# Two transformer blocks on one core: paired heads and earlier transposes in the sliding attention, another order of the dense products, no weight splits on GpSimd, and a paired operand for gate and up

## The chip, the cores and the metric

One NeuronCore of a Trainium2 chip runs the whole program in one launch. The metric is the device time of one execution in microseconds, the median of a few runs. The engines are named as in the profile: PE (TensorE, matrix products) with its weight loads as PEld, DVE (VectorE), ACT (ScalarE), POOL (GpSimd) and SP (SyncE, which issues the transfers).

## The reference, cut to what matters

The first block (a gated mixer with a delta rule, then a mixture of 32 experts) is not touched. The change lies in the second block: two layers, each an attention mixer with a residual and a SwiGLU with a residual, on 256 positions of width 1024.

```
for layer in range(2):
    hn = rmsnorm(h, attn_norm[layer])
    if layer % 2 == 0:   # 8 low-rank heads (96 wide, rotary) and 8 dilated heads (64 wide)
        mix = even_mixer(hn, e_w_in, e_q_norm, e_kv_norm, e_w_uq, e_w_ukv, e_w_out, ...)
    else:                # 16 query heads on 2 key heads (64 wide), window 128, one sink a head
        mix = odd_mixer(hn, o_w_qkv, o_sinks, o_w_out, ...)
    h = h + mix
    gu = rmsnorm(h, ffn_norm[layer]) @ w_gate_up          # 1024 -> 2 * 2816
    h = h + (silu(gu[..., :2816]) * gu[..., 2816:]) @ w_down
return rmsnorm(h, final_norm)
```

In the odd mixer, query heads 0 to 7 use key head 0 and query heads 8 to 15 use key head 1.

## The kernel before, in words

Everything is float32 in memory. For the dense products each operand is split into a high part, rounded to fp32r, and a low part, the remainder: `split` (L247) lets ACT write the high part and DVE (or another engine that it is given) subtract for the low part. A product is then three matmuls: high by high, high by low, low by high.

`dense` (L277) makes one such product. It fetches weights through SP in pieces of 2048 columns into `raw` (a ring of five), splits them 512 columns at a time into `wh` and `wl` (five buffers each, pool `sp`), and accumulates in one of two PSUM tiles `pd`. In mode "fm" the weights are the stationary operand and the 256 positions stream by: three matmuls of 256 columns (L309, L311, L312) for each 128 x 128 piece of weights. In mode "tm" the positions are stationary and 512 columns of weights stream by (L319 to L321). The argument `lo_eng` names another engine for some of the low parts; `block2` gives every fourth to POOL (`lo_p`).

`Norm` (L1162) turns a residual into transposed operands `xh` and `xl` (eight chunks of 128 features) and computes the reciprocal root mean square `rs` separately; `finish` also spreads it along a row (`rb`, matmuls L1196, copy L1199). The factor is applied only when a product leaves PSUM (`evac_row`, `evac_col`).

`attention` (L1201) works on four heads at a time. Two heads share a step: scores into PSUM (L1217), then on DVE, for each head and each half of the queries, scale and add the table of the mask (L1221, L1222) and take the maximum (L1223, L1224); ACT makes the exponentials with their sums (L1234); POOL normalizes the first 128 columns (L1241) and DVE the other 256 (L1242). The returned `out` does the rest for each pair of heads: three transposes a head (L1251), a copy out of PSUM on ACT (L1253), the products with the values (L1257), and a split. A plain f32 matmul shows in the trace as two matmuls.

`block2` puts it together. Even layer: the low-rank inputs `e_a` (416 columns), a chain of small steps on them (squares, a root, rotary, scaling, transposes L1379, splits), then dilated keys `e_b[0]`, low-rank keys, queries, scores of low-rank heads 0 to 3, their values, scores of heads 4 to 7, dilated queries `e_b[2]`, and the rest; dilated values `e_b[1]` and the first half of the output product `e_out` come behind the last scores. Odd layer: keys `o_kv` (256 columns, each key head twice, so that a query head in either half of the partitions finds its key beside it), values `o_v`, queries `o_q[0]`, scores, queries `o_q[1]`, and so on.

`ffn` (L1263) makes gate and up in eleven steps of 512 columns (256 of gate, 256 of up; mode "fm"), with the factor, the silu, the product and a split behind each, and then the down product in mode "tm".

The order of instructions on each engine is not written out: a scheduler fixes it when the program is built, from the order of the code, declared priorities and its own estimate of when operands are ready. Each engine then executes its own list in that order.

## Time and profile before

| what | us |
|---|---|
| three runs | 1402.52, 1404.14, 1411.59 (median 1404.14) |
| the profiled execution | 1411.76, of which the span is 1410.0 |
| PE busy in it | 1237.7 (88% of the span) |
| DVE, ACT, POOL busy in it | 722.3, 576.6, 122.1 |

The profile is of one execution. A busy time is the union of the instructions of an engine; the ends of matmuls are modelled, so the distance from one matmul's start to the next says more of the rate than its duration does. An idle time of an engine is put down to what released it last. Times of rows are counted from the start of the span.

### The profile page before, as it was taken

What the parts mean: (1) busy time and instruction counts of PE and PEld (TensorE: products, weight loads), DVE (VectorE), ACT (ScalarE), POOL (GpSimd) and SP (SyncE); (2) the same over time, 40 slices, a digit from 0 to 9 for tenths busy, and PEclk for the clock granted to TensorE, in tenths of its full rate; (3) what the DMA queues carried; (4) which work ended last, traced back from release to release, by engine and by line L of the source; (5) the groups of instructions that cost most, each with busy time, mean ns of one, the idle gap of its engine ahead of it and who ended that gap; (6) DMA issues with size and microseconds to landing.
All of it is one profiled execution on the core that took longest, in us unless ns stands there. A gap on an engine that the chain in (4) does not pass through costs nothing.

```text
span 1410.0 us, 26508 instructions
## 1 busy us (share of the span) xinstructions
PE 1237.7 (88%) x10876; PEld 1003.3 (71%) x10877; DVE 722.3 (51%) x1485; ACT 576.6 (41%) x1138; POOL 122.1 (9%) x108
## 2 busy tenths in 40 slices
PE   5999999999788666877777579999999999999997
PEld 4997988998555242443434268689998896999985
DVE  6997945886331010110100198666665668666664
ACT  3776534643211010110101156665555547655553
POOL 2431100030000000000000023300000014000000
PEclk9999988999899888888878789999999999999999
DMA  7453652687899999999999934335555542555550
GB/s 277 150 180 105 191 169 76 223 342 296 336 426 424 426 419 426 426 426 426 425 426 426 403 139 162 137 130 179 180 183 192 184 175 91 172 187 181 179 180 30
DMA packets 58973, 356.15 MB, mean 253 GB/s; under 512 B 13312, under 2 KB 13824, under 8 KB 17632
## 3 DMA queue, kind: packets, MB, share of 16 engines
q1 hardware_dynamic: 57072, 346.96, 64.5%
q0 software_dynamic: 1488, 6.92, 1.3%
q8 instruction: 87, 1.43, 0.4%
q10 hardware_dynamic: 288, 0.52, 0.1%
q14 instruction: 38, 0.31, 0.1%
HBM read 352.55 MB, written 1.84 MB: 251 GB/s over the span
## 4 chain that ended last, share of the span: by engine, by line
PE 36%; DMA 19%; DVE 5%; ACT 3%; issue 1%; POOL 1%; SPq 0%; DVEq 0%; ACTq 0%
DMA xw<-in_w_dram 15%; PE pd L311 7%; PE pd L312 7%; PE pd L309 7%; DMA raw<-in_w_dram 4%; PE pd L320 4%; PE pd L319 4%; PE pd L321 4%; ACT s L1234 1%; PE ps L1257 1%; DVE wl L249 1%; PE ps L1217 1%; PE ps L1251 1%; PE ps L1040 0%; PE ps L1025 0%
## 5 line engine op out<-in xcount | busy, mean ns | idle before, releaser
L248 ACT ACTIVATE wh<-raw 128x512 fp32r<-128x512 f32 (+1 forms) x532 | 330.8, 630 | 317.0 <-PE pd L311 166.6
L249 DVE TENSOR_TENSOR wl<-raw,wh 128x512 fp32r<-128x512 f32 x497 | 362.9, 738 | 182.8 <-ACT wh L248 181.8
L312 PE MATMUL pd<-xh,wl 128*128 128x256 f32 x1232 | 351.1, 285 | 3.9 <-DVE wl L249 2.3
L309 PE MATMUL pd<-xh,wh 128*128 128x256 f32 x1232 | 351.2, 285 | 0.4 <-ACT vn L737 0.4
L311 PE MATMUL pd<-xl,wh 128*128 128x256 f32 x1232 | 350.2, 284 | 0.0
L312 PEld LDWEIGHTS pd<-xh,wl 128*128 128x128 f32 x1232 | 236.8, 192 | 7.1 <-DVE wl L249 3.3
L309 PEld LDWEIGHTS pd<-xh,wh 128*128 128x128 f32 x1232 | 237.0, 192 | 3.0 <-issue 1.6
L311 PEld LDWEIGHTS pd<-xl,wh 128*128 128x128 f32 x1232 | 237.0, 192 | 1.6 <-issue 1.2
L1029 DVE COPY hs<-ps 128x256 f32<-128x256 f32 x32 | 13.6, 425 | 294.8 <-PE ps L1025 294.8
L1025 PE MATMUL ps<-xw,xe 128*32 128x256 f32 x1568 | 106.8, 405 | 36.6 <-DMA xw<-in_w_dram 32.7
L249 POOL TENSOR_TENSOR wl<-raw,wh 128x512 fp32r<-128x512 f32 (+1 forms) x35 | 57.6, 1646 | 636.9 <-ACT wh L248 616.1
L1025 PEld LDWEIGHTS ps<-xw,xe 128*32 128x32 f32 x1568 | 48.8, 115 | 88.1 <-DMA xw<-in_w_dram 47.1
L1035 ACT ACTIVATE hx<-ps 128x128 f32<-128x128 f32 x32 | 8.9, 277 | 244.3 <-PE ps L1032 244.3
L1040 PE MATMUL ps<-xw,hx 128*32 128x256 f32 x784 | 62.6, 457 | 21.6 <-DVE hx L1036 16.7
L320 PE MATMUL pd<-wl,hh 128*128 128x512 f32 x176 | 68.6, 390 | 0.0
L321 PE MATMUL pd<-wh,hl 128*128 128x512 f32 x176 | 68.6, 390 | 0.0
L319 PE MATMUL pd<-wh,hh 128*128 128x512 f32 x176 | 68.5, 389 | 0.0
L1040 PEld LDWEIGHTS ps<-xw,hx 128*32 128x32 f32 x784 | 24.4, 125 | 50.5 <-DVE hx L1036 23.1
L320 PE MATMUL pd<-wl,xh 128*128 128x512 f32 (+2 forms) x144 | 55.7, 387 | 2.5 <-DVE wl L249 2.5
L1047 PE MATMUL pd<-ys,owt 32*128 32x256 f32 x512 | 43.3, 459 | 16.2 <-ACT ys L1044 10.2
L321 PE MATMUL pd<-wh,xl 128*128 128x512 f32 (+2 forms) x144 | 54.3, 377 | 1.2 <-DVE xl L275 1.2
L319 PE MATMUL pd<-wh,xh 128*128 128x512 f32 (+2 forms) x144 | 54.7, 380 | 0.0
(451 smaller groups left out, 1750.4 us busy)
## 6 DMA issues: line engine op xcount, KB each, us to landing
xw<-in_w_dram SPq DMA_DIRECT2D x147, 1024.0 KB, 19.6
raw<-in_w_dram SPq DMA_DIRECT2D x45, 1024.0 KB, 19.6
raw<-in_gu_dram SPq DMA_DIRECT2D x44, 1024.0 KB, 5.1
raw<-in_w_in_dram SPq DMA_DIRECT2D x32, 1024.0 KB, 5.1
raw<-in_dn_dram SPq DMA_DIRECT2D x20, 1024.0 KB, 4.9
raw<-in_e_b_dram SPq DMA_DIRECT2D x6, 1024.0 KB, 5.1
bc<-in_big_dram POOLq DMA_DIRECT2D x8, 512.0 KB, 6.6
raw<-in_w_pb_dram SPq DMA_DIRECT2D x4, 1024.0 KB, 5.3
```

Source lines behind the costliest of these rows:

```text
L248: self.nc.scalar.activation(hi, src, AF.Copy)
L249: (eng or self.nc.vector).tensor_tensor(lo, src, hi.bitcast(F32), op=OP.subtract)
L309: nc.tensor.matmul(o, a, xh[:, kc, :], start=(kc == 0 and oc % 2 == 0), stop=False, skip_group_check=True)
L311: nc.tensor.matmul(o, a, xl[:, kc, :], start=False, stop=False, skip_group_check=True)
L312: nc.tensor.matmul(o, b, xh[:, kc, :], start=False, stop=(kc == nk - 1), skip_group_check=True)
L319: nc.tensor.matmul(o, xh[:, kc, ts], a, start=(kc == 0), stop=False, skip_group_check=True)
L320: nc.tensor.matmul(o, xh[:, kc, ts], b, start=False, stop=False, skip_group_check=True)
L321: nc.tensor.matmul(o, xl[:, kc, ts], a, start=False, stop=(kc == nk - 1), skip_group_check=True)
L1025: T.matmul(ph[32 * c:32 * c + 32, :256], xe[:, kc, ei * 32:ei * 32 + 32], wt[kc // 2][:, kc % 2, c * 256:(c + 1) * 256], start=(kc == 0), ...
L1040: T.matmul(py[32 * c:32 * c + 32, :256], hx[:, fc % 2, (fc // 2) * 32:(fc // 2) * 32 + 32], wt[4 + fc // 2][:, fc % 2, c * 256:(c + 1) * 2 ...
L1047: T.matmul(total(c, t), owt[32 * c:32 * c + 32, ei, t * 128:(t + 1) * 128], ys[32 * c:32 * c + 32], start=(e == 0 and t == 0), stop=(e == ...
L1217: T.matmul(ps[:, t * 128:t * 128 + 128 * (t + 1)], q[:, t * 128:t * 128 + 128], k[:, :128 * (t + 1)], start=(t == 0 and j == 0), stop=(j = ...
```

## The change

In the feed-forward step, the normalized operand is stored with its high and low parts side by side for each chunk (`x2`, a new pool), and a new mode "fm2" streams both, 512 columns, past the high weights in one matmul, and the high part alone, 256 columns, past the low weights. Gate and up are made in 22 steps of 256 columns. The two halves of the wide sum are joined when they leave PSUM: ACT copies one, DVE adds the other. Weights are split 1024 columns at a time, with three buffers of each kind instead of five, through the down product too.

In the even layer the order becomes: dilated keys (left in PSUM), low-rank inputs, the row of the factor, dilated queries, then the low-rank chain; dilated values stand where dilated queries stood. In the odd layer the first queries come ahead of keys and values, and the sixteen heads are reordered as 0, 8, 1, 9, ..., so that both heads of a pair use different key heads and the keys need only 128 columns. No weight split goes to POOL in this block. In `attention` the maxima of two heads are one instruction each, the second normalization goes from DVE to ACT, the transposes of the next pair stand ahead of the products of this one, one of two copies out of PSUM goes to DVE, and the products of a pair alternate between the halves of the array in another order. The end of the expert stage no longer makes the row of the factor.

```diff
@@ layout
+PAIRED = np.arange(16).reshape(2, 8).T.ravel()
...
-    o["o_kv"] = _tiles(w, [np.concatenate([r(1024, 1088), r(1024, 1088), r(1088, 1152), r(1088, 1152)])], 8)[0]
+    o["o_k"] = _tiles(w, [r(1024, 1152)], 8)[0]
@@ dense
-        step = max(1, 512 // ncol)
+        step = max(1, self.wide // ncol)
...
-                wh = self.sp.tile([128, 512], F32R, name="wh", tag="wh")
-                wl = self.sp.tile([128, 512], F32R, name="wl", tag="wl")
+                wh = self.sp.tile([128, self.wide], F32R, name="wh", tag="wh")
+                wl = self.sp.tile([128, self.wide], F32R, name="wl", tag="wl")
...
+                    if mode == "fm2":
+                        for oc in range(ncol // 128):
+                            c = c0 + oc * 128
+                            nc.tensor.matmul(ps[:, oc * 512:(oc + 1) * 512], wh[:, c:c + 128],
+                                             xh[:, kc].rearrange("p a b -> p (a b)"), start=(kc == 0), stop=False,
+                                             skip_group_check=True)
+                            nc.tensor.matmul(ps[:, oc * 512:oc * 512 + 256], wl[:, c:c + 128], xh[:, kc, 0], start=False,
+                                             stop=(kc == nk - 1), skip_group_check=True)
@@ end of moe
-                x.finish()
+                x.finish(False)
@@ attention
-                V.tensor_reduce(mx[:, 0, i:i + 1], s[:, i, :128], AX.X, OP.max)
-                V.tensor_reduce(mx[:, 1, i:i + 1], s[:, i, 128:], AX.X, OP.max)
+            V.tensor_reduce(mx[:, 0, i0:i0 + wide], s[:, i0:i0 + wide, :128], AX.X, OP.max)
+            V.tensor_reduce(mx[:, 1, i0:i0 + wide], s[:, i0:i0 + wide, 128:], AX.X, OP.max)
...
-            V.tensor_scalar(s[:, i, 128:], s[:, i, 128:], den[:, 1, i:i + 1], None, op0=OP.mult)
+            S.activation(s[:, i, 128:], s[:, i, 128:], AF.Copy, scale=den[:, 1, i:i + 1])
...
+        def turned(i2):
...
+                if i == i2:
+                    S.activation(d, pp[:, :384], AF.Copy)
+                else:
+                    V.tensor_copy(d, pp[:, :384])
...
+            nxt = turned(0)
             for i2 in range(0, n, 2):
+                pT, nxt = nxt, turned(i2 + 2) if i2 + 2 < n else None
...
-                for kb in range(2):
-                    for i in (i2, i2 + 1):
-                        r = slice(64 * (i - i2), 64 * (i - i2) + 64)
-                        T.matmul(po[r, kb * 128:256], vv(heads[i], kb), pT[i][:, kb * 256:256 + kb * 128], start=(kb == 0),
-                                 stop=(kb == 1), skip_group_check=True)
+                for i, kb in ((0, 1), (1, 0), (0, 0), (1, 1)):
+                    T.matmul(po[64 * i:64 * i + 64, kb * 128:256], vv(heads[i2 + i], kb), pT[i][:, kb * 256:256 + kb * 128],
+                             start=(kb != i), stop=(kb == i), skip_group_check=True)
@@ ffn
+        sp, self.wide = self.sp, 1024
+        with tc.tile_pool(name="ffn", bufs=1) as fp, tc.tile_pool(name="ffw", bufs=2) as fw, \
+                tc.tile_pool(name="ffs", bufs=3) as self.sp:
...
-            for s in range(11):
+            for s in range(22):
...
+                    lo = self.work.tile([128, 2, 256], F32, name="tf", tag="tf")
+                    nc.scalar.activation(lo, p2[:, :, 1], AF.Copy)
+                    nc.vector.tensor_tensor(gu[0][:, :, s % 2], p2[:, :, 0], lo, op=OP.add)
...
-                self.dense(A[f"gu{i}"][s], 512, 8, x.xh, x.xl, "fm", act)
+                self.dense(A[f"gu{i}"][s], 256, 8, x.x2, None, "fm2", act)
@@ block2, even
+                pk = self.dense(A["e_b"][0], 512, 8, x.xh, x.xl, "fm", None)
...
-                self.dense(A["e_a"], 416, 8, x.xh, x.xl, "tm", self.evac_col(ca[:, :, :416], x.rs), lo_p)
+                self.dense(A["e_a"], 416, 8, x.xh, x.xl, "tm", self.evac_col(ca[:, :, :416], x.rs))
+                x.row()
+                self.evac_row(kb, x.rb)(pk)
+                qb = self.x2.tile([128, 8, 256], F32, name="qb", tag="x2")[:, :4]
+                self.dense(A["e_b"][2], 512, 8, x.xh, x.xl, "fm", self.evac(qb))
...
-                self.dense(A["e_b"][0], 512, 8, x.xh, x.xl, "fm", self.evac_row(kb, x.rb), lo_p)
...
-                self.dense(A["e_b"][2], 512, 8, x.xh, x.xl, "fm", self.evac(qb), lo_p)
+                self.dense(A["e_b"][1], 512, 8, x.xh, x.xl, "tm", self.evac_col(vb, x.rs))
...
-                self.dense(A["e_b"][1], 512, 8, x.xh, x.xl, "tm", self.evac_col(vb, x.rs), lo_p)
@@ block2, odd
-                self.dense(A["o_kv"], 256, 8, x.xh, x.xl, "fm", self.evac_row(kk, x.rb), lo_p)
-                self.dense(A["o_v"], 128, 8, x.xh, x.xl, "tm", self.evac_col(vs, x.rs), lo_p)
-                self.dense(A["o_q"][0], 512, 8, x.xh, x.xl, "fm", self.evac(q[:, :4]), lo_p)
+                self.dense(A["o_q"][0], 512, 8, x.xh, x.xl, "fm", self.evac(q[:, :4]))
+                self.dense(A["o_k"], 128, 8, x.xh, x.xl, "fm",
+                           lambda ps: V.tensor_tensor(kk, ps[:, :256], x.rb, op=OP.mult))
+                self.dense(A["o_v"], 128, 8, x.xh, x.xl, "tm", self.evac_col(vs, x.rs))
```

## Rows read from the trace of the kernel before

**Rows 1.** Windows: length, then busy us of PE, PEld, DVE, ACT, POOL; clock; DMA

```profile
814.60:933.40 118.80, 107.36 (x663) 90.34 (x664) 91.63 (x218) 72.46 (x183) 33.70 (x29) 0.98 0.39 135
815.00:860.00 45.00, 38.06 (x254) 35.65 (x253) 43.06 (x98) 23.53 (x51) 11.69 (x6) 0.95 0.48 171
933.40:1061.70 128.30, 128.09 (x1068) 127.87 (x1067) 84.58 (x138) 71.94 (x117) 0.00 (x0) 1.00 0.54 181
1061.70:1122.30 60.60, 60.60 (x275) 50.21 (x274) 34.78 (x53) 31.87 (x54) 0.00 (x0) 1.00 0.53 182
1122.30:1210.90 88.60, 85.76 (x583) 71.09 (x582) 61.92 (x168) 54.95 (x150) 24.25 (x26) 1.00 0.41 144
```

**Rows 2.** Waits of PE in 812 to 935: total us, times, longest

```profile
PE ps L1196 <- DVE rs L1192: 2.1, 1, 2.1
PE ps L1379 <- DVE ca L1367: 1.6, 1, 1.6
PE pd L312 <- POOL wl L249: 1.6, 1, 1.6
PE pd L309 <- DVE kb L1317: 1.2, 1, 1.2
PE pd L320 <- POOL wl L249: 0.8, 1, 0.8
PE ps L1257 <- ACT pT L1253: 0.8, 1, 0.8
```

**Rows 3.** Waits of PE in 1121 to 1215, the same columns

```profile
PE ps L1257 <- ACT pT L1253: 1.5, 2, 0.8
```

**Rows 4.** Windows of PE alone, inside gate and up, and inside down

```profile
960.00:1050.00 90.00, 90.00 (x752) 1.00 0.56 186
1100.00:1120.00 20.00, 20.00 (x90) 1.00 0.57 197
```

**Rows 5.** Chain of work that ended last, even layer: start us, us, what

```profile
817.73 0.57 ACT xh L271
...
833.85 0.62 ACT ca L1325
...
841.54 0.30 PE ps L1379
...
856.32 2.62 PE ps L1217 x16
```

**Rows 6.** Timeline of PE around one pair of heads: start us, us, instruction, idle before

```profile
1167.50 1.24 PE L1257 MATMUL ps<-pT,vs 128*64 128x256 f32 x8 [0.81 <-ACT pT L1253]
1168.67 0.87 PE L1251 MATMUL ps<-cst,s 128*128 128x128 f32 x6
```

**Rows 7.** Timeline, a split on POOL and the VectorE instruction beside it

```profile
830.60 1.36 POOL L249 TENSOR_TENSOR wl<-raw,wh 128x512 fp32r<-128x512 f32 x1 [1.09 <-ACT wh L248]
...
830.72 1.26 DVE L218 TENSOR_SCALAR nr_y<-nr_t 128x2 int32<-128x2 int32 x1
```

**Rows 8.** Groups by line, whole span: busy us, mean ns of one, idle before

```profile
L249 DVE TENSOR_TENSOR wl<-raw,wh 128x512 fp32r<-128x512 f32 x497 | 362.9, 738 | 182.8 <-ACT wh L248 181.8
L248 ACT ACTIVATE wh<-raw 128x512 fp32r<-128x512 f32 (+1 forms) x532 | 330.8, 630 | 317.0 <-PE pd L311 166.6 <-DVE wl L249 72.2 <-PE pd L321 54.8
L1242 DVE TENSOR_SCALAR s<-s,den 128x256 f32<-128x256 f32 x32 | 11.0, 405 | 0.2
L1253 ACT ACTIVATE pT<-ps 128x384 f32<-128x384 f32 x32 | 14.3, 486 | 7.2 <-PE ps L1251 6.9
L1014 ACT ACTIVATE owt<-ps 128x512 f32<-128x512 f32 x16 | 9.6, 597 | 1.1
L807 DVE TENSOR_TENSOR tf<-pd,ga 128x512 f32<-128x512 f32 x4 | 2.6, 687 | 0.4 <-PE pd L312 0.4
L1071 DVE TENSOR_TENSOR acc<-acc,bc 128x1024 f32<-128x1024 f32 x2 | 2.4, 1214 | 0.0
L885 ACT ACTIVATE h<-h,nmean,nr_y 128x1024 f32<-128x1024 f32 x2 | 2.4, 1232 | 1.9 <-DVE nmean L878 1.9
```

More of the change, by code (lines that the diff above doesn't have):

```diff
@@ L125, in layout @@
             ("norm", g["dn_norm_w"][0]), ("b_r", np.concatenate([g["b_rg"][0], g["b_re"][0]])),
-            ("sink", g["o_sinks_2"][0])]
+            ("sink", g["o_sinks_2"][0][PAIRED])]
     n = 0
@@ L322, in dense @@
                                              skip_group_check=True)
-        if k_to == nk:
+        if k_to == nk and consume is not None:
             consume(ps)
@@ L376, in run @@
             self.work = pool("work", 2)
-            self.sp = pool("sp", 5)
+            self.sp, self.wide = pool("sp", 5), 512
+            self.x2 = pool("x2")
             self.block2(x, n)
@@ L385, in mixer @@
         sp_es = ExitStack()
-        self.sp = sp_es.enter_context(tc.tile_pool(name="sp", bufs=5))
+        self.sp, self.wide = sp_es.enter_context(tc.tile_pool(name="sp", bufs=5)), 512
         self.ln_norm(h, h, 1e-5)
@@ L1165, with __init__ @@
     class Norm:
-        def __init__(self, p, h, gain):
+        def __init__(self, p, h, gain, paired=False):
             self.p, self.h, self.gain = p, h, gain
-            self.xh = p.act.tile([128, 8, 256], F32R, name="xh", tag="xh")
-            self.xl = p.act.tile([128, 8, 256], F32R, name="xl", tag="xl")
+            if paired:
+                self.x2 = p.x2.tile([128, 8, 2, 256], F32R, name="x2", tag="x2")
+                self.xh, self.xl = self.x2[:, :, 0], self.x2[:, :, 1]
+            else:
+                self.xh = p.act.tile([128, 8, 256], F32R, name="xh", tag="xh")
+                self.xl = p.act.tile([128, 8, 256], F32R, name="xl", tag="xl")
             self.ss = p.small.tile([128, 2, 2], F32, name="nss", tag="nss")
@@ L1193, in finish, with row @@
             if row:
-                ps = p.pt.tile([128, 512], F32, name="ps", tag="ps")
-                for t in range(2):
-                    nc.tensor.matmul(ps[:, t * 128:(t + 1) * 128], self.rs[:, t:t + 1].to_broadcast([128, 128]),
-                                     p.cs("ident"), start=True, stop=True, skip_group_check=True)
-                self.rb = p.small.tile([128, 256], F32, name="rb", tag="rb")
-                nc.vector.tensor_copy(self.rb, ps[:, :256])
+                self.row()
+        def row(self):
+            p, nc = self.p, self.p.nc
+            ps = p.pt.tile([128, 512], F32, name="ps", tag="ps")
+            for t in range(2):
+                nc.tensor.matmul(ps[:, t * 128:(t + 1) * 128], self.rs[:, t:t + 1].to_broadcast([128, 128]),
+                                 p.cs("ident"), start=True, stop=True, skip_group_check=True)
+            self.rb = p.small.tile([128, 256], F32, name="rb", tag="rb")
+            nc.vector.tensor_copy(self.rb, ps[:, :256])
     def attention(self, heads, qk, vv, tab, scale, oh, ol, sink=None, wide=2):
@@ L1285, in ffn @@
                     done(s)
+        self.sp, self.wide = sp, 512
         if nx is not None:
@@ L1332, in block2 @@
         ident, small = self.cs("ident"), self.small
-        lo_p = lambda i: P if i % 4 == 3 else None
         if True:
@@ L1367, in block2 @@
                     V.tensor_scalar(ca[:, t, 256:384], ca[:, t, 256:384], rs[:, 2 * t + 1:2 * t + 2], None, op0=OP.mult)
-                cxh = ev.tile([128, 3, 256], F32R, name="cxh")
-                cxl = ev.tile([128, 3, 256], F32R, name="cxl")
+                cx = ev.tile([128, 2, 3, 256], F32R, name="cx")
+                cxh, cxl = cx[:, 0], cx[:, 1]
                 krT = ev.tile([128, 256], F32, name="krT", tag="kr")
@@ L1389, in block2 @@
                 va = ev.tile([128, 2, 512], F32, name="va")
-                kb = ev.tile([128, 4, 256], F32, name="kb")
                 vb = ev.tile([128, 2, 512], F32, name="vb", tag="ca")
-                qb = ev.tile([128, 4, 256], F32, name="qb")
                 oxh = ev.tile([128, 8, 256], F32R, name="oxh")
@@ L1444, in block2 @@
                 d1 = att_d(1)
-                self.dense(A["e_b"][1], 512, 8, x.xh, x.xl, "tm", self.evac_col(vb, x.rs), lo_p)
-                po = [self.dense(A["e_out"][s], 512, 8, oxh, oxl, "tm", None, lo_p, (0, 4)) for s in range(2)]
+                po = [self.dense(A["e_out"][s], 512, 8, oxh, oxl, "tm", None, ks=(0, 4)) for s in range(2)]
                 d0()
@@ L1460, in block2 @@
                 P.dma_start(tab.rearrange("p a b -> p (a b)"), A["tab_swa"])
-                kk = ev.tile([128, 2, 256], F32, name="kk")
+                kk = ev.tile([128, 256], F32, name="kk")
                 vs = ev.tile([128, 2, 128], F32, name="vs")
@@ L1488, in block2 @@
                 a3 = att(3)
-                po = [self.dense(A["o_out"][s], 512, 8, oxh, oxl, "tm", None, lo_p, (0, 4)) for s in range(2)]
+                po = [self.dense(A["o_out"][s], 512, 8, oxh, oxl, "tm", None, ks=(0, 4)) for s in range(2)]
                 a2()
                 a3()
-                y = self.Norm(self, h, self.par("ffn_norm1"))
+                y = self.Norm(self, h, self.par("ffn_norm1"), True)
                 for s in range(2):
-                    self.dense(A["o_out"][s], 512, 8, oxh, oxl, "tm", self.residual(h, s), lo_p, (4, 8), po[s])
+                    self.dense(A["o_out"][s], 512, 8, oxh, oxl, "tm", self.residual(h, s), None, (4, 8), po[s])
                     y.part(s)
```

63 lines of the change are left out of this document (35 added, 28 removed).

## The prediction

> **What bounds the kernel now.** I read the windows by stage first, then the waits of PE in the two attention stages, then the rate of PE inside one long product, and last the chain of waits at the start of the even layer. The reader is to see this. The second block runs from 814.6 to about 1400 and PE is its bound nearly everywhere: gate and up take 128.3 us with PE busy for 128.1, down 60.6 with 60.6, and only the even attention leaves PE a tenth idle (107.4 of 118.8); in the odd one it is busy 85.8 of 88.6 [rows 1]. The clock is full there (0.98 to 1.00). So time can be won in two ways only: less work for PE, or fewer of the waits of PE, which are listed [rows 2, 3]. The transfers take 0.38 to 0.54 of the queues and stand in none of these waits. A second engine is near: in the first 45 us of the even layer VectorE is busy 43.1 of 45 [rows 1], though part of that is not work. While POOL makes a low part, the VectorE instruction beside it lasts as long as POOL's: an operation on two columns took 1.26 us beside a split of 1.36 [rows 7].
>
> **The paired operand.** Steady gate and up start 750 matmuls of 256 columns in 90 us, when the two that straddle the edges are left out: 0.120 us each. Down starts some 88 of 512 columns in 20 us: 0.227 each [rows 4]. The columns alone would make the second twice the first; it is 0.013 short of that, so each matmul of this kind carries about 13 ns that do not grow with its columns. A piece of weights cost 3 x 0.120 = 0.360 and will cost 0.227 + 0.120 = 0.347. There are 8 x 44 pieces in a layer and two layers, 704 in all: **9.4 us saved**. The bounds: nothing, if the wide matmul over two halves runs at the rate per column of the 256-column ones (0.120 / 256); 14 us, if everything ran at the rate per column of the wide ones (768 columns x 0.227 / 512 = 0.340). I take 9.4, since the row for 512 columns is the same kind of matmul. The page "TensorE: Matmul & The Clock Gate" of the Trainium skill (Back-to-back issue gap) speaks against the gain: it puts a matmul at its columns at full clock plus 2.5 ns, so that dropping one of three would be worth some 704 x 2.5 ns = 1.8 us, an estimate from that page. The trace disagrees on the level, 0.120 where the page has 0.109.
>
> The price lies beside it. Each of the 44 steps adds a copy on ACT of 512 columns out of PSUM (0.597) and an addition on VectorE (0.687); the splits become 44 a layer of 1024 columns at 1.21 to 1.23 instead of 88 at 0.738 and 0.630 [rows 8]. VectorE goes from 84.6 to 84.6 + 15.1 - 64.9 + 53.4 = 88 us a layer, ACT from 71.9 to 71.9 + 13.1 - 55.4 + 54.2 = 84, both under the 124 that PE will need. I cost them at nothing, with PE as the cover. If that cover fails, it is a rival below.
>
> At the start of gate and up something is lost. The first product starts on chunks 0 to 3 while the norm of chunks 4 to 7 is still being made. That cover was 48 matmuls, 5.8 us; now it is 16 in the same step, 4 x 2 x 0.347 = 2.8 us, unless the scheduler pulls the next step forward. The first split is also 1024 wide (0.6 + 0.5 us more), and its buffer is new: in the even layer it may lie where the output product's operand was, and then waits for the end of that product. I take 1 us a layer, **2 us lost** (bounds 0 and 5).
>
> **Keys of 128 columns.** 8 chunks x 1 piece x 3 matmuls fall away, 24 x 0.120 = **2.9 us saved**, certain as PE's work.
>
> **The order of a pair's products.** From the first product to the next transposes a pair takes 1.17 us [rows 6]. The two heads use different halves of the array, but the second head's first matmul comes behind the first head's wide ones. With a narrow one first it can start earlier, by about 0.1 us, a tenth of the pair's time: with 16 pairs **1.7 us saved**. The bounds are 9.4 (half of 1.17, as if one head's products lay wholly beside the other's) and a loss of 1.7, as much as I take, since no row shows the new order. The columns and weights are the same in both, so I stay near nothing.
>
> **Transposes ahead.** Waits for the copies out of PSUM are 0.8 us in the even layer and 1.5 in the odd [rows 2, 3]. Six transposes (0.65 us) or four products now cover a copy of 0.486, and half of the copies leave ACT. I take **2 us saved** of 2.3 (bounds 0 and 4, since waits under 0.15 us are not listed). The second normalization (0.405, 32 times) moves 13 us from VectorE to ACT, 16 copies the other way, and the maxima become fewer instructions on the same elements; both engines go on beside PE, and I cost this at nothing. Without that cover it is in rival (b).
>
> **The order in the even layer.** Now the first operand is ready at 818.3, the low-rank inputs leave PSUM at 833.9 and scores begin at 856.3, 22.5 us later [rows 5]. PE waits 2.1 us for the factor, 1.6 for the transposes and 1.2 for the keys' copy [rows 2]; of the 6.9 us that it idles between 815 and 860 [rows 1] that leaves 2.0 for first operands and low parts, which I keep. After: dilated keys (96 x 0.120 = 11.5) come first, then the low-rank inputs (48 matmuls of 416 columns, at the rate of the wide ones 9 us): 818.3 + 11.5 + 9 + 2.0 = 841. The low-rank chain then puts scores at 841 + 22.5 = 863.5. PE has to make in that time the row and wait for the keys' copy, which holds the next PSUM tile (2.3), dilated queries (11.5), transposes (0.9), low-rank keys and queries (60 matmuls, 7.2): 862.9. So the chain ends last, by little, and scores come 7.2 later than now, with 11.5 us of dilated queries already done: **4.3 us saved**. The bounds are 0 (the scheduler follows readiness and gives the order of now, or VectorE is late with its 8 more splits in that stretch) and 9 (PE's waits there all vanish). Dilated values take the place of dilated queries behind the low-rank scores and cost what they cost now.
>
> What is late next is the softmax of the last heads. Only half of the output product (48 x 0.227 = 10.9 us) stands behind the last scores, where that and dilated values, 21.8, stood; and ACT has more normalizing ahead of its copies. I take **1.5 us lost** there and in the odd layer's tail (bounds 0 and 4).
>
> **No splits on POOL.** PE waited 1.6 + 0.8 us for POOL's low parts [rows 2]: **2.4 us saved**. The 21 splits cost VectorE 21 x 0.738 = 15.5 us, and it is rid of up to 21 blocked instructions of about a microsecond each [rows 7]; I count that as even. At the end of the expert stage five splits stand among the small steps of a norm that PE waits for; one was POOL's and is now VectorE's, 0.738: **0.7 us lost** (bounds 0 and twice that).
>
> **The sum** against the profiled execution: 1411.8 - 9.4 - 2.9 - 1.7 - 2.0 - 4.3 - 2.4 + 2.0 + 1.5 + 0.7 = 1393.3, 18.5 less. That execution is 7.6 above the median of the runs shown, 1404.1; so the forecast in terms of the median is 1404.1 - 18.5 = 1386.
>
> **The rivals.** (a) Attention goes further: the even order's waits vanish (9 us), the products gain half of their bound (4.7) and nothing is lost at starts and tails. That is 9.4 + 2.9 + 4.7 + 2.3 + 9 + 2.4 = 30.7, so 1373. For it: PE is all that the windows show as full. Against it: VectorE at 43.1 of 45.
> (b) VectorE and ACT set the attention stages, and all that I save there but the narrow keys comes back as waits for low parts and softmax. 18.5 - 1.7 - 2.0 - 4.3 - 2.4 = 8.1, so 1396. For it: 43.1 of 45, and 91.6 of 118.8 over the even layer. Against it: part of VectorE's time is blocking by POOL.
> (c) The wide matmul costs by its columns as the narrow ones do, and gate and up gain nothing: 18.5 - 9.4 = 9.1, so 1395. For it: no row has a matmul that streams two operands at once. Against it: the wide ones of down start every 0.227 us, not 0.240. By the rate of the page named above, the Trainium skill's, it would be 18.5 - 9.4 + 1.8 = 10.9, 1393, an estimate on the same side.
> (d) Slower: the wide splits starve PE. A block of four chunks lasts PE 16 matmuls, 2.8 us; with three buffers a split has 5.5 us from the release of its buffer. ACT and VectorE need 1.23 + 1.21 and some 0.2. It decides from 2.9 us of other work ahead of it in their lists; each 0.4 us more is paid 88 times, 35 us, so 1386 + 35 = 1421. For it: the five other VectorE instructions of a pair of steps add up to 5 x 0.687 = 3.4. Against it: they depend on ACT's in turn and do not come in one block.
>
> **How the numbers follow.** A measurement of this kernel tells about 1% from no change, so the lines are 1390 and 1418. My forecast has 0.60, and its own range 1378 to 1394 puts 0.50 of that under 1390; (a) has 0.13, (b) 0.13, (c) 0.07, (d) 0.07. Faster: 0.50 + 0.13 and 0.05 from the lower parts of (b) and (c), 0.68. Slower: 0.07, from (d). The same: the rest, 0.25. The range from 1370 to 1400 takes in (a), (b) and (c) and leaves out (d) and the ends.
>
> **What would show it.** In gate and up: starts of 0.227 and 0.120 in turn, and a stage shorter by 4.7 us; waits of PE for `wl` there speak for (d). In the even layer: scores near 863 us and no wait for the factor or the keys' copy; a full VectorE with waits for `wl` speaks for (b). The POOL waits must be gone, and no small VectorE instruction should last a microsecond except beside the copies that POOL keeps. I am wrong if the down product or the expert stage, whose work is the same, moves by more than a microsecond or two.

## The result and the profile after

The changed kernel takes 1395.11 us (median of 8 runs, 1387.71 to 1398.57), the kernel before 1408.11 beside it (1402.52 to 1413.42): a ratio of 0.9892 over the runs, with an interval of 0.987 to 0.9914 (the two medians alone give 0.9908). It is faster by about 1%, and in the forecast range, but 9 us above the forecast of 1386. Of these, 4.0 lie in the base (1404.14 was the median of the runs shown, 1408.11 that of the runs beside the change). The profiled executions differ by 1411.76 - 1398.57 = 13.2 us where the sum said 18.5.

Windows of the kernel before, with edges at the last matmul of one product and the first or last of the next; length, then busy us of PE, PEld, DVE, ACT, POOL, clock, DMA share, GB/s. The stages are the even layer, gate and up, down, the odd layer, gate and up:

```profile
818.19:933.17 114.98, 103.57 (x648) 86.96 (x646) 87.82 (x214) 70.23 (x180) 33.70 (x29) 0.99 0.40 139
933.17:1061.93 128.76, 128.54 (x1070) 128.29 (x1069) 85.03 (x138) 71.94 (x117) 0.00 (x0) 1.00 0.54 180
1061.93:1122.51 60.58, 60.58 (x273) 50.16 (x272) 34.55 (x52) 31.87 (x54) 0.17 (x1) 1.00 0.53 183
1122.51:1210.83 88.32, 85.48 (x582) 70.84 (x580) 61.85 (x168) 54.95 (x150) 24.09 (x26) 1.00 0.41 144
1210.83:1339.57 128.74, 128.53 (x1071) 128.28 (x1070) 85.02 (x138) 71.94 (x117) 0.00 (x0) 1.00 0.54 180
```

The same stages of the changed kernel:

```profile
817.31:926.61 109.30, 104.18 (x647) 88.76 (x646) 83.59 (x197) 70.06 (x184) 13.32 (x18) 0.97 0.39 134
926.61:1054.72 128.11, 126.91 (x719) 109.31 (x717) 92.75 (x116) 73.00 (x96) 0.00 (x0) 1.00 0.52 181
1054.72:1115.30 60.58, 60.58 (x274) 50.16 (x272) 33.19 (x35) 28.22 (x36) 0.00 (x0) 1.00 0.57 191
1115.30:1200.08 84.78, 81.19 (x558) 68.39 (x556) 60.40 (x148) 56.72 (x154) 10.98 (x17) 0.98 0.42 140
1200.08:1326.33 126.25, 126.25 (x719) 109.40 (x717) 89.18 (x113) 70.41 (x93) 0.00 (x0) 1.00 0.52 182
```

The 13.2 us lie here: 0.9 ahead of the block, 5.7 in the even layer, 0.65 and 2.5 in gate and up, 3.5 in the odd layer, nothing in down and the end. One profiled execution of each kernel stands behind these lengths, and the granted clock is not the same in both: 0.97 in the changed kernel's even layer and 0.98 in its odd one, against 0.99 and 1.00. What that is worth is worked out below. The forecast had 7.4 in the two gate and up stages together (9.4 less 2); they gave 3.15. VectorE did not become full there (92.75 of 128).

The rate is the first thing to read. PE's timeline inside gate and up of the changed kernel (start us, us, instruction), the answer to [rows 4]:

```profile
990.06 0.40 PE L310 MATMUL pd<-x,wh 128*128 128x512 f32 x1
990.29 0.28 PE L313 MATMUL pd<-x,wl 128*128 128x256 f32 x1
990.41 0.40 PE L310 MATMUL pd<-x,wh 128*128 128x512 f32 x1
990.65 0.28 PE L313 MATMUL pd<-x,wl 128*128 128x256 f32 x1
990.77 0.40 PE L310 MATMUL pd<-x,wh 128*128 128x512 f32 x1
```

From wide to narrow 0.23 or 0.24, from narrow to wide 0.12; by the raw starts the median steps are 236 and 117 ns, and a piece takes 353.3, not 347. That is 6.7 ns saved a piece and not 13.4: 704 x 6.7 ns = 4.7 us.

The second thing is the start of the first gate and up stage. ACT's timeline there (in brackets the idle time ahead of an instruction and what ended it):

```profile
923.71 0.87 ACT L269 ACTIVATE x<-ps,prm 128x256 fp32r<-128x256 f32 x2 [0.19 <-DVE x L270]
927.09 1.06 ACT L250 ACTIVATE wh<-raw 128x1024 fp32r<-128x1024 f32 x1 [2.51 <-PE pd L332]
```

The first wide split waits 2.5 us for the last matmul of the output product, as it would if the new buffer lies where that product's operand was. The first matmul of gate and up comes 1.6 us behind the output product's last (926.61 to 928.20).

The waits of PE in the even layer of the changed kernel (total us, times, longest), to be held against [rows 2]:

```profile
PE pd L322 <- DVE xl L277: 1.7, 1, 1.7
PE pd L320 <- DVE ka L1450: 1.2, 1, 1.2
PE pd L320 <- DVE ca L1365: 1.1, 1, 1.1
PE pd L330 <- ACT wh L250: 0.4, 1, 0.4
PE ps L1424 <- DVE tf L1427: 0.4, 1, 0.4
PE pd L331 <- DVE wl L251: 0.2, 1, 0.2
```

The waits for the factor, for POOL's low parts and for the keys' copy are gone. No VectorE instruction on 64 columns or fewer lasts over 0.7 us in the block any more (5 did before, beside POOL's splits as in [rows 7]). The wait for the first operand's low part was there before too (1.2); new are waits for PSUM tiles that VectorE empties. Scores begin at 865.9; the forecast had 863.5.

### The profile page after: what moved, and what is told of

Its sections match the earlier page's. It is cut to its first block, busy times and chain, and to the rows that moved or that the text cites. A ratio compares the mean times of both kernels' runs of the same rounds, so it can differ in the third digit from the quotient of the medians.

```text
span 1396.8 us, 24576 instructions
## 1 busy us (share of the span) xinstructions
PE 1230.9 (88%) x10146; PEld 966.6 (69%) x10149; DVE 725.2 (52%) x1368; ACT 570.9 (41%) x1064; POOL 87.9 (6%) x87
## 5 line engine op out<-in xcount | busy, mean ns | idle before, releaser
L251 DVE TENSOR_TENSOR wl<-raw,wh 128x512 fp32r<-128x512 f32 (+2 forms) x384 | 351.1, 926 | 168.1 <-ACT wh L250 167.0
L250 ACT ACTIVATE wh<-raw 128x512 fp32r<-128x512 f32 (+2 forms) x398 | 302.1, 771 | 318.2 <-PE pd L332 90.3
L310 PE MATMUL pd<-x,wh 128*128 128x512 f32 x704 | 249.5, 399 | 0.0
L313 PE MATMUL pd<-x,wl 128*128 128x256 f32 x704 | 198.2, 282 | 0.4 <-DVE wl L251 0.4
L310 PEld LDWEIGHTS pd<-x,wh 128*128 128x128 f32 x704 | 132.4, 188 | 33.0 <-DVE x L270 0.2
L320 PE MATMUL pd<-xh,wh 128*128 128x256 f32 x520 | 150.9, 290 | 3.1 <-ACT wh L250 1.6
L323 PE MATMUL pd<-xh,wl 128*128 128x256 f32 x520 | 150.3, 289 | 2.3 <-DVE wl L251 2.3
L322 PE MATMUL pd<-xl,wh 128*128 128x256 f32 x520 | 149.6, 288 | 1.7 <-DVE xl L277 1.7
L313 PEld LDWEIGHTS pd<-x,wl 128*128 128x128 f32 x704 | 133.2, 189 | 1.0 <-DVE wl L251 1.0
L320 PEld LDWEIGHTS pd<-xh,wh 128*128 128x128 f32 x520 | 101.7, 196 | 6.3 <-issue 2.3
L323 PEld LDWEIGHTS pd<-xh,wl 128*128 128x128 f32 x520 | 101.5, 195 | 4.9 <-DVE wl L251 3.3
L322 PEld LDWEIGHTS pd<-xl,wh 128*128 128x128 f32 x520 | 101.6, 195 | 3.0 <-DVE xl L277 2.0
```

What stands on the lines that cost most here:

```text
L250: self.nc.scalar.activation(hi, src, AF.Copy)
L251: (eng or self.nc.vector).tensor_tensor(lo, src, hi.bitcast(F32), op=OP.subtract)
L310: nc.tensor.matmul(ps[:, oc * 512:(oc + 1) * 512], wh[:, c:c + 128], xh[:, kc].rearrange("p a b -> p (a b)"), start=(kc == 0), stop=False, ...
L313: nc.tensor.matmul(ps[:, oc * 512:oc * 512 + 256], wl[:, c:c + 128], xh[:, kc, 0], start=False, stop=(kc == nk - 1), skip_group_check=True)
L320: nc.tensor.matmul(o, a, xh[:, kc, :], start=(kc == 0 and oc % 2 == 0), stop=False, skip_group_check=True)
L322: nc.tensor.matmul(o, a, xl[:, kc, :], start=False, stop=False, skip_group_check=True)
```

## Experiments: gate and up

All experiments edit the changed kernel. I give the lengths of its four stages as above: even, gate and up, odd, gate and up (changed kernel: 109.30, 128.11, 84.78, 126.25).

**Gate and up as before.** `self.wide` stays 512, `ffn` and its weights' layout are the old ones.

> The changed kernel with gate and up as before (blocks of 512 columns, three matmuls of 256 columns per piece, splits of 512 columns out of the five old buffers); all else as changed. Theory: the paired operand is worth what the stages' marks say, about 0.7 us in the first feed-forward layer and 2.5 us in the second (from the last instruction of the output product to the first of the down product), so this kernel is about 3 us slower than the changed one, with the steady pace back at 0.360 us per piece against 0.353. Rival: the stages' marks hide something that the paired operand costs elsewhere (in the attention layers through its 16 KB, or at the stage ends), and this kernel is as fast as the changed one or faster. By the prediction's own term (9.4 less 2) it would be 7 us slower.

1400.02 us, ratio to before 0.9913 (0.9885 to 0.994). The stages: 107.62, 128.74, 84.64, 128.75, the pace 360.0 ns. The paired operand is worth 0.6 and 2.5 us, 3.1 in all, as the marks said. The even layer got 1.7 shorter with no edit there; that is told below.

**Splits of 512 columns out of the old buffers.**

```diff
-        sp, self.wide = self.sp, 1024
...
-                tc.tile_pool(name="ffs", bufs=3) as self.sp:
...
-        self.sp, self.wide = sp, 512
```

> The changed kernel with the paired operand kept, but its weights split 512 columns at a time out of the five old buffers instead of 1,024 columns out of three new ones. Theory that the start of the stage loses by the wide splits: TensorE's idle time in the first 6 us of each gate and up stage falls by 1 to 2 us, the steady pace stays 0.353 us per piece, and each stage is 1 to 2 us shorter. Rival, the wide splits are needed: twice as many split instructions with their fixed cost put ScalarE or VectorE behind TensorE, which would show stalls of TensorE on wh or wl in the steady part and a stage as long as with the wide splits, or longer. Rival, the start loss comes from the rows of the norm and not from the splits: no difference, within 0.5 us per stage.

1392.13 us, ratio 0.9866 (0.9843 to 0.9889); stages 109.27, 126.20, 83.89, 123.98. The first gate and up stage is 1.9 us shorter, and its first matmul comes 0.23 us behind the output product's last. This edit changes the splits' width and their buffers together; that the loss was the buffer's place, and not the width, follows from the second stage of the changed kernel, where the first matmul comes 0.23 us behind (1200.08 to 1200.31) with the wide splits. There is no wait for a split in the steady part, so the wide splits are not needed. The second stage surprised. Windows of PE in its steady part and in that of the first (columns as above):

```profile
1215.00:1305.00 90.00, 90.00 (x521) 78.68 (x520) 70.42 (x108) 58.25 (x100) 0.00 (x0) 1.00 0.53 188
945.00:1035.00 90.00, 90.00 (x511) 77.99 (x510) 68.28 (x105) 56.38 (x96) 0.00 (x0) 1.00 0.53 187
```

One program, one order of instructions, one clock: 521 matmuls in 90 us in the one stage, 511 in the other. By the raw starts a piece takes 346.7 ns in the second stage and 353.3 in the first, each from the last stall at the start to the end. At 346.7 the stage is 4.76 us shorter than before, which is what the forecast had for it.

**Wide matmuls in a row, narrow ones behind them.**

```diff
+                    jobs = [(b0 + k0 + kk, oc, kk * ncol + oc * 128) for kk in range(kn) for oc in range(ncol // 128)]
+                    for kc, oc, c in jobs:
+                        nc.tensor.matmul(ps[:, oc * 512:(oc + 1) * 512], wh[:, c:c + 128],
...
+                    for kc, oc, c in jobs:
+                        nc.tensor.matmul(ps[:, oc * 512:oc * 512 + 256], wl[:, c:c + 128], xh[:, kc, 0], start=False,
```

> The changed kernel, where the eight matmuls of 512 columns that a split feeds are issued in a row and its eight of 256 columns behind them, instead of in turn. Theory that the turn between widths is what costs: the wide ones start every 0.227 us and the narrow ones every 0.120, as in the streams of one width of the kernel before, 0.347 per piece, so that each stage is 352 x 0.006 = 2.2 us shorter, and some more at the start, since the first eight matmuls need the high halves alone. Rival, it is the price of the form: the wide ones with a weight tile as stationary operand start every 0.236 whatever comes ahead of them, the narrow ones every 0.117 to 0.120, 0.353 to 0.356 per piece, and the stages are as long as in the changed kernel.

> Both edits together: splits of 512 columns out of the old buffers, and the four wide matmuls of a split ahead of its four narrow ones. If both the start and the turn cost, the two gains add: 3 to 4 us less per stage than in the changed kernel, 6 to 8 us in all, and the steady pace is about 0.349 us per piece (a change of width twice in eight matmuls instead of every time). If neither does, the time is that of the changed kernel.

The first: 1390.68 us, ratio 0.9856 (0.9816 to 0.9897), stages 109.35, 125.81, 83.88, 124.86, pace 349.1 in both stages. The second: 1388.85 us, 0.9851 (0.9815 to 0.9887), 107.62, 125.71, 84.57, 125.69, pace 350.8 in both. In a row of eight the wide steps are 233, 236, 228, 233, 231, 226, 227, 227 ns, the narrow ones 113, 119 and then 120. So neither theory held in full: it is not the form (the row comes down to 227), and not the turn alone (the first five wide ones behind a change are late). The two gains of the second kernel did not add.

**Starting again within the stage.** Behind every fourth block VectorE does twelve needless additions, so that PE runs out of split weights.

> The changed kernel with twelve needless VectorE additions of 512 columns behind every fourth block of gate and up, so that TensorE runs out of split weights and starts again five times more in each stage (the stage is some 20 us longer for it; the output is unchanged). So far one and the same stream of wide and narrow matmuls ran at 353.3 ns per piece in nine stages and at 346.7 in three, each from its last stall to the stage's end. Theory that the start after a stall chooses the pace: between stalls the pace is constant, and over the twelve stretches both values occur, 346.7 in some and 353.3 in most. Rival, the pace belongs to the place of the buffers or to the stage (so far the first stage has always had 353.3): all stretches of a stage have one pace.

The kernel was run once: 1408.42 us. By the marks the stages came to 130.93 and 129.16, but here the last pieces of gate and up come behind the first matmuls of down; gate and up with down are 6.6 and 6.7 us longer than in the changed kernel, where 20 a stage were expected. PE stopped as meant. The pace of each stretch, from the raw starts of L310 and L313; in most stretches a second disturbance of some 80 ns (172 in the second stretch), about 40 pieces in, parts it:

```
start of the stretch, us    ns per piece    behind the second disturbance
 934.74                     353.3
 959.63                     346.6, then 353.3 with no gap between   353.3
 983.58                     353.3           353.3
1007.57                     353.3           346.7
1031.56                     353.3           346.7
1211.30                     353.3
1237.69                     353.3           353.3
1261.68                     353.3           346.7
1285.68                     353.3           346.7
1309.68                     353.3           346.7
```

Both values occur in both stages, so the pace belongs neither to the stage nor to a place of the buffers that is fixed for a stage. The theory holds in part: of the ten starts one ran at 346.7; behind the seven small disturbances of some 80 ns the pace had changed five times, and held for the 15 or so pieces up to the next; once it changed with no gap at all. Over the other eight kernels that take the two widths in turn, 12 stages ran at 353 and 4 at 347 from their last stall on, and all four were second stages. What fixes the pace is open.

## Experiments: attention

**The products' half as before** (transposes beside their own products, ScalarE copies all, old order), and **the order of the four products alone.**

```diff
-                for i, kb in ((0, 1), (1, 0), (0, 0), (1, 1)):
+                for i, kb in ((0, 0), (1, 0), (0, 1), (1, 1)):
```

> The changed kernel with the products' half of attention as before: a pair's transposes stand right ahead of its products, the products go key block by key block, ScalarE copies every transposed tile. The changed kernel takes 109.3 us for the even layer (first dense product to last output product) and 84.8 us for the odd one (end of the down product to end of the output product). Theory, by the prediction's terms of 1.7 for the order and 2.0 for the transposes: both layers together 3 to 4 us longer, and waits of the products for pT of about 0.8 us per pair are back in the trace. Rival, the other changes have already covered these waits or moved them elsewhere: both layers within 1 us of the changed kernel. Rival, the order is worth its upper bound of 9.4: 9 us or more.

> The changed kernel with one thing undone: the four products of a pair go key block 0 for both heads and then key block 1 for both, instead of block 1, 0, 0, 1. Theory by the prediction's term: 16 pairs x 0.1 us, 1.7 us longer over both layers. Rival, no difference, within 0.5 us: two products on different column groups run beside one another in either order. Rival, the order was the larger part of the attention's gain: 5 us or more.

The whole half: 1403.75 us, ratio 0.996 (0.9934 to 0.9986), even 111.91, odd 91.06: 8.9 us longer in the two layers, more than twice the theory's 3 to 4 and just short of the 9 that the last rival named. The order alone: 1393.86 us, 0.9909 (0.9877 to 0.9941), even 109.46, odd 86.02: 1.4 longer, the term of 1.7.

**Transposes not ahead, all else new.**

```diff
-            nxt = turned(0)
...
-                pT, nxt = nxt, turned(i2 + 2) if i2 + 2 < n else None
+                pT = turned(i2)
```

> The changed kernel where a pair's transposes are issued right ahead of its own products instead of one pair ahead; the copies stay shared by ScalarE and VectorE and the products keep the new order. The kernel with the whole old half took 111.9 us for the even layer and 91.1 for the odd one, against 109.3 and 84.8. Theory that issuing them ahead is what carries: 6 to 8 us of these 8.9 are here too. Rival, the loss came from giving ScalarE all copies beside its new normalisation: within 2 us of the changed kernel over both layers, with the waits of the products for pT short. By the prediction's own term: 2.0 us longer.

1401.77 us, 0.9956 (0.9932 to 0.9979), even 112.83, odd 90.09: 8.8 longer; the ratios, 0.9956 against 0.9892, say the same. So issuing the transposes ahead carries the whole of it: with that undone, the old order and the old copies add nothing more. PE's waits in the odd layer (total, times, longest):

```profile
PE pd L320 <- ACT wh L250: 2.5, 1, 2.5
PE ps L1285 <- ACT pT L1273: 1.2, 1, 1.2
```

In the changed kernel the first of these is 1.6 and the second is not there. By the steps from one matmul's start to the next, the 5.3 us of the odd layer are 2.1 behind transposes (these two waits), 1.1 behind a pair's products, 1.4 behind matmuls of the output product and 0.9 behind scores; in the even layer the steps behind transposes are 2.4 longer. So more than half of the odd layer's part lies in steps too short to be listed as waits.

The 8.8 us are what the transposes are worth beside the other edits. Without them the odd layer takes 90.09 us, some 0.9 of it the clock (below), and so still more than the 88.32 of the kernel before, though it has 24 matmuls fewer. So some of the other edits lengthen the layer, and the transposes ahead make up for it. What they would be worth alone in the kernel before, no run shows.

**The normalization on VectorE again.**

```diff
-            S.activation(s[:, i, 128:], s[:, i, 128:], AF.Copy, scale=den[:, 1, i:i + 1])
+            V.tensor_scalar(s[:, i, 128:], s[:, i, 128:], den[:, 1, i:i + 1], None, op0=OP.mult)
```

> The changed kernel where the wide part of each head's softmax is multiplied by the reciprocal on VectorE again and not on ScalarE. Theory by the prediction's term (1.5 us lost by the move, since ScalarE's instruction is the longer one): 1 to 2 us shorter over both layers. Rival, with the low halves of all splits on VectorE it is the fuller engine by now, and the move is what makes room: 2 us or more longer, with waits of TensorE for VectorE's results (wl, pT, s).

1389.54 us, 0.9875 (0.9819 to 0.9932), even 106.64, odd 83.22. The odd layer is 1.6 shorter, the even one 2.7; against the same layers at an equal clock, below, it is 0.7 and 1.0, together 1.7, the theory's 1 to 2. ACT's timeline of the changed kernel shows a wait that the move made:

```profile
1152.17 1.69 ACT L1262 ACTIVATE s<-s,den 128x256 f32<-128x256 f32 x4
...
1156.01 0.61 ACT L250 ACTIVATE wh<-raw 128x512 fp32r<-128x512 f32 x1
```

and PE, at the same place, waits for that split:

```profile
1156.67 0.39 PE L320 MATMUL pd<-xh,wh 128*128 128x256 f32 x1 [1.61 <-ACT wh L250]
```

Four normalizations, 1.7 us, stand in ACT's list among the exponentials, ACT is never idle for some 12 us, and the split that PE waits for is behind them. With the normalization on VectorE this wait is gone.

**Splits on POOL again**, every fourth one in both layers.

> The changed kernel with every fourth split's low half on GpSimd again in both attention layers. Theory by the prediction's term: waits of TensorE for wl from GpSimd are back, and small VectorE instructions beside GpSimd's take 1.0 to 1.3 us instead of 0.1 to 0.7; both layers together 2 to 3 us longer. Rival, VectorE is the tighter engine in the attention layers by now and GpSimd's help is worth more than the waits: both layers together as long or shorter.

1398.72 us, 0.9915 (0.9889 to 0.9942), even 109.90, odd 86.46: 2.3 longer, the term of 2.4 (3.2 at an equal clock, below). PE waits for POOL's low parts again, 0.6 us in the even layer and 0.5 in the odd, and four VectorE steps on 8 columns or fewer last 1.06 to 1.25 us, where none lasts over 0.7 in the changed kernel.

**The even layer's order as before.**

```diff
-                pk = self.dense(A["e_b"][0], 512, 8, x.xh, x.xl, "fm", None)
+                x.row()
...
-                self.dense(A["e_b"][2], 512, 8, x.xh, x.xl, "fm", self.evac(qb))
```

(and `e_b[0]`, `e_b[2]`, `e_b[1]` at their old places.)

> The changed kernel with the even layer's dense products in the order of before: the norm's row ahead of all, e_a, then the keys e_b[0] behind the rotary stage, the queries e_b[2] ahead of the first heads' products, the values e_b[1] behind the last scores. Theory by the prediction's term: the waits for the factor (2.1 us), for the copy of ca (1.6) and for the scores' softmax are back and the even layer takes 3 to 5 us longer than 109.3. Rival, the layer is bound elsewhere (by VectorE's and ScalarE's work of the heads) and the order only moves the wait: within 1 us. The odd layer stays at 84.8.

1388.5 us, 0.9867 (0.9819 to 0.9915), even 106.10, odd 84.63. Neither theory: the old order is 3.2 us *faster*. PE's waits there:

```profile
PE pd L332 <- DVE xl L277: 1.2, 1, 1.2
PE pd L320 <- DVE kb L1356: 0.9, 1, 0.9
PE pd L331 <- DVE wl L251: 0.8, 1, 0.8
PE pd L322 <- DVE cx L251: 0.4, 1, 0.4
PE ps L1421 <- DVE ca L1409: 0.3, 1, 0.3
PE ps L1270 <- DVE s L1242: 0.3, 1, 0.3
PE pd L323 <- DVE wl L251: 0.2, 1, 0.2
PE ps L1216 <- DVE rs L1208: 0.2, 1, 0.2
```

The waits that the new order was to remove are small in the old order too: the factor 0.2 (2.1 in [rows 2]), `ca` 0.3 (1.6). The matmuls that wait for the factor, in the kernel before and in this one:

```profile
833.91 0.68 PE L1196 MATMUL ps<-cst,rs 128*128 128x128 f32 x4 [2.10 <-DVE rs L1192]
```

```profile
830.63 0.68 PE L1216 MATMUL ps<-cst,rs 128*128 128x128 f32 x4 [0.19 <-DVE rs L1208]
```

Both start 15.72 us behind the first product (818.19 and 814.91). So the factor comes no earlier, although no small VectorE step lies beside a split on POOL any more; but 73 matmuls instead of 57 stand ahead of it in PE's list, the 16 more being products of the keys. `ca` comes 0.5 us earlier. Whether the missing splits on POOL or another edit moved these matmuls forward is not isolated. From the first product to the first scores this kernel takes 35.2 us (814.9 to 850.1), the kernel before 38.0 (818.2 to 856.2).

Some of the 3.2 is the clock. Windows of the changed kernel, and of the one with gate and up as before, 2.3 us behind the first product of the even layer:

```profile
819.60:821.60 2.00, 2.00 (x9) 2.00 (x10) 2.00 (x5) 0.00 (x0) 0.00 (x0) 0.50 0.00 0
```

```profile
821.10:823.10 2.00, 2.00 (x17) 2.00 (x18) 2.00 (x5) 0.52 (x1) 0.00 (x0) 1.00 0.03 8
```

In 12 us that end 2 us ahead of the first product PE was busy for 2.90 and 3.47, and it comes out of that at 0.50, the lower level. In the changed kernel it stays there (1.2 GHz) for 16 more matmuls, of 213 ns instead of 120: 1.5 us, and 0.2 in the two beside them. In the other kernel, with the same instructions, the third matmul already runs at full speed. Of the eleven kernels with the new order, seven ran the slow stretch and four did not (prod_old had it later); the four have even layers of 107.6, 107.6, 107.6 and, with VectorE's normalization, 106.6. The old order never had it in three. So of the 3.2 us 1.7 go with this clock (109.3 against 107.6) and 1.5 with the order (107.6 against 106.1). That the order causes the slow clock is not shown.

The odd layer has such a stretch too. Two 4 us windows of the changed kernel, behind the wait of 1.6 us for a split that is shown above, and the whole odd layer of the kernel with splits of 512 columns:

```profile
1155.30:1159.30 4.00, 2.62 (x14) 2.28 (x14) 2.81 (x8) 4.00 (x13) 1.13 (x2) 0.83 0.24 41
1159.30:1163.30 4.00, 4.00 (x31) 2.86 (x31) 2.36 (x6) 2.96 (x8) 1.92 (x3) 0.74 0.53 221
```

```profile
1112.51:1196.40 83.89, 79.95 (x558) 67.16 (x556) 60.07 (x151) 56.59 (x156) 11.02 (x17) 1.00 0.42 151
```

Seven kernels have this odd layer unedited. Five fell to the lower clock in it and take 84.6 to 84.8 us; two did not and take 83.9, with the same wait. So 0.9 us of the changed kernel's 84.78 are the clock. Neither the wait nor the fall is there with VectorE's normalization; that the one brings the other is not shown, since splits on POOL left the wait and the clock stayed full. The kernels with the normalization on VectorE and with splits on POOL have an odd layer at the full clock, so theirs are to be held against 83.9.

**The three together:** old even order, normalization on VectorE, wide matmuls in a row.

> The changed kernel with the three edits together that took time off it one by one: the even layer's dense products in the order of before, the wide part of the softmax multiplied on VectorE, and the wide and narrow matmuls of a split of gate and up in two rows instead of in turn. If the edits add: even layer 105 to 106.5 us instead of 109.3, odd layer 83 to 84 instead of 84.8, feed-forward stages 125.8 and 124.9 instead of 128.1 and 126.3, 7 to 10 us less than the changed kernel and a ratio to the kernel before near 0.983. If VectorE becomes too full with both attention edits at once, the even layer is longer than 107 and the sum 5 us or less. The pace of gate and up is 349 ns per piece in both stages, since no other has been seen for this order.

1388.31 us, ratio to before 0.9841 (0.9807 to 0.9874). Its windows by stage, without down, columns as above:

```profile
816.83:922.73 105.90, 101.68 (x648) 87.11 (x646) 88.18 (x213) 64.83 (x168) 14.91 (x18) 0.99 0.43 151
922.73:1048.48 125.75, 124.97 (x719) 109.45 (x718) 92.45 (x116) 73.68 (x97) 0.00 (x0) 1.00 0.52 185
1109.07:1192.26 83.19, 81.39 (x558) 67.50 (x557) 65.03 (x164) 50.03 (x138) 11.40 (x17) 1.00 0.43 148
1192.26:1317.24 124.98, 124.95 (x719) 109.33 (x718) 89.26 (x113) 70.96 (x94) 0.00 (x0) 1.00 0.51 180
```

Each stage is where it was expected, 8.6 us less than the changed kernel in all; 2.6 of them are the clock of the two attention layers (1.7 and 0.9), at which the changed kernel was profiled. By ratios it is half a per cent ahead of the changed kernel, with intervals that overlap a little.

## Why the prediction was right, and where it was not

| term, us saved | forecast | measured |
|---|---|---|
| paired operand, steady | 9.4 | 4.7 (9.4 at the other pace) |
| start of gate and up | -2.0 | -1.6 |
| keys of 128 columns | 2.9 | 2.9 (24 matmuls fewer, x582 to x558) |
| order of a pair's products | 1.7 | 1.4 |
| transposes ahead | 2.0 | 8.8 |
| order of the even layer | 4.3 | -1.5 at equal clock, -3.2 as profiled |
| no splits on POOL | 2.4 | 3.2 at equal clock, 2.3 as profiled |
| softmax and tail (the moved normalization) | -1.5 | -1.7 at equal clock, -4.2 as profiled |
| end of the expert stage | -0.7 | -0.6 (PE's wait 7.9, now 8.5) |

**By parts.** The forecast had 7.4 us for gate and up and 11.8 for the two attention layers (2.9 + 1.7 + 2.0 + 4.3 + 2.4 - 1.5). Gate and up gave 3.15. The layers gave 9.2 as profiled and 11.8 at equal clock (7.4 and 4.4). That the second figure meets the forecast is luck: two of its terms are far off, in opposite directions, and the parts do not add, as the next paragraphs say.

**Right.** The direction; the bound (PE); the start loss with its place (the new buffer) and size, though it fell on one layer whole; the keys, the order of products, the POOL splits, the moved normalization; down unchanged. Rival (d), PE starved by the wide splits, did not occur: the steady part has no wait for a split.

**Against the rivals.** The median of 1395.1 is nearer to the numbers of (b) and (c), 1396 and 1395, than to 1386, and the drop of 13.0 us lies between their 8.1 and 9.1 and the forecast's 18.5. As a mechanism (c) came true by half, in gate and up. (b) did not: the attention layers gained 9.2 us where it leaves 1.4. The line of 1% that the prediction drew at 1390 (1394 by the base measured beside the change) the median does not pass; the ratio of 0.9892 just does. (The prediction reads the transfers as 0.38 to 0.54 of the queues; its rows say 0.39 to 0.54, which changes nothing.)

**Mis-sized: the paired operand.** The step that gave 0.227 + 0.120 took the steps of streams of one width. In turn they hold at one of two paces, and in the profiled execution both stages ran at the slower one. The forecast's 346.7 is real: it is the other pace. By the Trainium skill's page "TensorE: Matmul & The Clock Gate" (Back-to-back issue gap), whose 2.5 ns beyond the columns are its figure for a matmul by itself, a piece would take 325 ns and the gain would be 1.8 us, an estimate from that page; the runs show 347 to 353 and 4.7 to 9.4.

**Wrong in size: the transposes.** 2.0 was taken from waits that are listed in the kernel before, with bounds to 4. Taken back, they cost 8.8. The bound was too narrow for two reasons: it held only waits that are listed, where more than half of the odd layer's part lies in shorter steps, and it priced them in the kernel before, where the other edits had not yet lengthened the layer.

**Wrong in sign: the even order.** The step credited it with 2.1 + 1.6 + 1.2 us of waits. The kernel without it has hardly any of the first two, and 0.9 of the third: other parts of the change had covered them already, as 16 more products ahead of the factor show. Which part did is not isolated. The step credited to one part waits that another removes as well.

**Not additive.** The single undoings of the even layer come to about 2 at equal clock (3.5 + 0.2 + 0.6 - 1.0 - 1.5), while it gained 7.4 at that clock; those of the odd layer to 11.3 with the keys (5.3 + 1.2 + 2.6 - 0.7 + 2.9), while it gained 4.4. The scheduler lays out the whole block anew for each edit. What gave the other 5 to 6 us of the even layer was not isolated; candidates are the joined maxima and POOL's absence in the old layout. The sum came as near as it did because errors of opposite sign met in it: 6.8 too little for the transposes, against 4.7 too much for the operand and 5.8 for the order.

## What to carry to other kernels

A wait listed in a profile belongs to its cause and not to the first edit that would cover it: before crediting a reordering with a wait, ask which other part of the change removes it. Price a stream of mixed instructions by a mixed stream, since the steps of pure ones are its best case. Where one part of a bundle is taken back alone, look at each stage's length and granted clock and not only at the total, and expect the parts not to add: here 2.5 of the 4.2 us that one undoing seemed to gain were the clock of the execution that was profiled.

## What the hardware showed

One stream of matmuls of 512 and 256 columns in turn, at the full clock and with no wait, ran at 353.3 or at 346.7 ns a pair for over 100 us; behind five of seven gaps of some 80 ns it had changed from the one to the other. In rows of eight, wide matmuls behind narrow ones start 228 to 236 ns apart for the first five and 226 to 227 after that. The same instructions at the start of the even layer ran at the lower clock for 16 matmuls in some executions and at the full one in others, 1.5 us apart; behind a wait of 1.6 us in the odd layer it fell to the lower clock in five kernels of seven with that layer unedited, which cost 0.7 to 0.9 us.
